# Time mixing of a two-layer model: from a scheduler's order to one written order for TensorE, VectorE, ScalarE and GpSimd

## The chip, the cores and the metric

The kernel runs on one core of a Trainium2 chip. The metric is the device time in microseconds (us) of one launch: 773.28 us is the median of three runs before the change (772.45, 773.28, 775.1). PE is TensorE, DVE is VectorE, ACT is ScalarE, POOL is GpSimd, and SP is the queue that issues the DMAs. A launch computes the whole model once, and all weights come from DRAM as float32 during it.

## The reference

The model has two layers over 256 tokens of width 1024 (16 heads of 64): layer 0 is block attention, layer 1 is RWKV-7 time mixing, each is followed by a gated feed-forward layer of width 2816, and a norm ends the program. The change is in time mixing only:

```python
xx = x_prev - x
xr, xw, xk, xv, xa, xg = [x + xx * mu[n] for n in range(6)]
r, k, v = xr @ w_r, xk @ w_k, xv @ w_v
w = -softplus(-(w0 + tanh(xw @ w1) @ w2)) - 0.5
decay = exp(-exp(w))
a = sigmoid(a0 + (xa @ a1) @ a2)
g = sigmoid(xg @ g1) @ g2
kk = k * k_k;  kk = kk / max(sqrt(sum(kk * kk)), 1e-12)     # per head
k = k * (1 + (a - 1) * k_a)
# per token t and head:
sa = state @ -kk_t
state = state * decay_t + outer(sa, kk_t * a_t) + outer(v_t, k_t)
y_t = state @ r_t
# then, per head
yn = (y - mean) * rsqrt(var + eps) * lnx_w + lnx_b
out = ((yn + sum(r * k * r_k) * v) * g) @ w_o
```

The kernel does not step through the tokens. It takes two chunks of 128 tokens, builds the triangular matrix T of products of decayed keys for every head and chunk, inverts I + T, and obtains the states and outputs by matrix products.

## The kernel before

Activations lie feature-major: a tile `x[:, kt]` is 128 features by 256 tokens, and there are eight of them. A weight piece of 128 x 1024 float32 (512 KB) is loaded by SP into `raw` and split exactly into a high and a low float32r part, the high one by ACT and the low one by DVE (`pieces`, `split_act`, both recorded as L133). A product with split operands is three matmuls (`mm3`, L137 to L139). Small projections run as plain float32 matmuls, which PE does in two passes; the trace has a record for each.

`rwkv` is the whole of time mixing. In the order of its code:

- for every contraction tile kt: the shifted and normed input `xn` (L449), its difference `xx` (L451), mixes of the two (L432), the key products (L137 to L139), the first halves of the low-rank projections for decay and rate (L463) and for the gate (L466), and the mixed value input;
- the second halves (L502, L503), the decays by a running sum (L510) and Exp (L587, L588), the key norms (squares L578, sums over a head L562, root L581, `spread` back over the head L569, directions L599), the products T (`prod`, L530, copied out by L533), the gate (L616), the values (L137 to L139, copied by L634);
- the inverses of 32 x 32 blocks of I + T: ACT and DVE gather the diagonal blocks (L649, L650), DVE transposes them (L651), and 31 steps of two DVE operations substitute (L655, L657), all heads and chunks at once;
- `state`: transposes back (L668, L670), scatters (L673, L674), corners of blocks of 32 and then of 64 (L683 to L715), means taken off the values (L726), X = M V (L747), token-major keys (L758), the two chunks (L768 to L789), the receptance r (L802, plain float32, 64 matmuls on unsplit weights), its products with keys (RK) and rates (RB) through `prod` with a mask (L536), the bonus (L822 to L835), the outputs (L852);
- `norm`, for two pairs of heads at a time: the remaining output products (L862 with U and RB, L864 with the state S1 and r), squares, sums, root, spread, gate and bonus, and a split; then the output projection.

A scheduler sets the order of instructions on each engine. It takes what is ready, and is guided by `issue_after` (do not place this before that) and by `weave`, which steps several generators in turn. Each engine then runs its own row strictly in that order. Weights of `wk` are loaded ahead during the last blocks of the feed-forward layer (`keys_ahead`).

Tiles come from pools with few slots: `b` has 15 general slots, `wp` 4 for split pieces, `rawp` 4, and PSUM has 4 slots `acc`, 2 `pt` and 2 `pu`. A writer waits until the slot's last reader is done.

Of the kernel before, what the change touches and what calls it, by code (L numbers as in the profile page):

```python
# [8 lines left out]
F32 = mybir.dt.float32  # L9
# [8 lines left out]
NB = 15  # L18
# [4 lines left out]
# columns of the packed vectors  # L23
# [8 lines left out]
# columns of the packed constants  # L32
# [31 lines left out]


class Trunk:
# [17 lines left out]
    def table(self, func, after):  # L84
        """have the activation table of func loaded once after is there, ahead of its use"""
# [14 lines left out]
    def t1(self, name="t1"):  # L100
        return self.wk.tile([128, S], F32, name=name, tag="t1", bufs=4)
# [12 lines left out]
    # ---- weights: raw float32 from DRAM, split exactly into two float32r parts  # L114
# [3 lines left out]
    def pieces(self, dram, n, own=0, after=False, fine=0):  # L118
        """dram [n/2, 128, 2048] -> n split pieces of [128, 1024], as a generator; the last own ones in general slots,
        the first fine ones in two steps"""  # L120
        for i in range(n):
            raw = self.raw()
            t = (self.b if i >= n - own else self.wp.tile)([128, 2, 1024], F32R, name="whl")
# [17 lines left out]
    # ---- the residual stream, feature-major; what the next sub-layer needs of it  # L141
# [28 lines left out]
    def rstd_tok(self):  # L170
        """1/rms of every token, tokens on partitions"""
# [12 lines left out]
    def rstd(self):  # L184
        """1/rms of every token, the same on all partitions (in PSUM)"""
# [7 lines left out]
    def out_proj(self, w, gname, split=True):  # L193
        """generator: h += w.T z; send (zhi, zlo) once per contraction tile"""
# [26 lines left out]
    # ---- layer 0: causal attention  # L221
# [15 lines left out]
    def attention(self, nxt="ffn0"):  # L237
# [55 lines left out]
        def soft(j):  # L293
            """heads 2j and 2j + 1"""
# [68 lines left out]
    # ---- gated convolutional feed-forward  # L363
    def ffn(self, l, nxt, split=True, ahead=iter(())):
# [30 lines left out]
        for fo in range(KT):  # L395
            ps = self.acc([128, S])
            for f in range(FT):
                if blk % 8 == 0:
                    hi, lo = next(w)
                    if blk >= 56 and blk % 16 == 8:  # L400
# [8 lines left out]
    # ---- layer 1: RWKV-7 time mixing  # L409
    def keys_ahead(self):  # L410
        for w in self.pieces(self.a["wk"], KT, own=KT, after=True):
            self.ahead.append(w)
            yield

    def rwkv(self, nxt="ffn1"):
        nc, a, tc = self.nc, self.a, self.tc
        mm = nc.tensor.matmul
        ident, head, sel = self.c("ident"), self.c("head"), self.c("sel", 0, 2)
# [3 lines left out]
        nc.sync.dma_start(l1[:, 1], a["g1"])  # L422
        omk = self.wk.tile([128, KT], F32, name="omk", bufs=1)
# [18 lines left out]
        # keys and the first halves of the low-rank projections, one contraction tile after the other  # L442
        xk = hilo()
        pk = []
        pwa, pg = self.pt([128, S]), self.pu([128, S])
        l2 = xv = None
        for kt in range(KT):
            with tc.issue_after(first[0].ins) if kt == 1 else nullcontext():
                nc.vector.scalar_tensor_tensor(xn[:, kt, 1:], self.h[:, kt], self.v("mix1", kt), rs,  # L449
                                               op0=OP.mult, op1=OP.mult)  # L450
            nc.vector.tensor_sub(xx[:, kt], xn[:, kt, :S], xn[:, kt, 1:])  # L451
            first = mix2(xk, 2, kt)
            for fo in range(KT):
                if kt == 0 and fo % 2 == 0:
                    pk.append(self.acc([128, 2, S]))
                f = slice(fo * 128, fo * 128 + 128)
# [7 lines left out]
            t = self.t1("mx")  # L464
            mix(t, 5, kt)
            mm(pg, lhsT=l1[:, 1, kt], rhs=t, start=kt == 0, stop=kt == 7)  # L466
            if kt == 0:
                l2 = self.b([128, 2, D], name="l2")
                nc.sync.dma_start(l2[:, 0], a["w2a2"])
                nc.sync.dma_start(l2[:, 1], a["g2"])  # L470
                xv = hilo()
            split = mix2(xv, 3, kt)
            if kt == 3:
                cut = split
        wv = self.pieces(a["wv"], KT)
        with tc.issue_after(cut[1].ins), tc.issue_after(cut[2].ins):
            wv0 = [next(wv) for _ in range(4)]

        # decay and in-context rate
        lt = self.wk.tile([128, S], F32, name="lt", bufs=1)  # L480
        nc.scalar.activation(lt[:64], pwa[:64], AF.Tanh)
        nc.scalar.copy(lt[64:], pwa[64:])
        gt = self.wk.tile([128, S], F32, name="gt", bufs=1)
        nc.scalar.activation(gt, pg, AF.Sigmoid)
        KK = self.b([128, KT, S], name="KK")
        for p in range(4):
            nc.vector.tensor_copy(KK[:, 2 * p:2 * p + 2], pk[p])
        A = self.b([128, KT, S], name="A")
        cm = self.b([128, KT, 2, C + 1], name="cm")
        nc.gpsimd.memset(cm[:, :, :, 0:1], 0.0)  # L490
# [497 lines left out]
```

## Time and profile before

| what | us |
|---|---|
| median of three runs (772.45 to 775.1) | 773.28 |
| span of the profiled execution, first to last instruction | 759.3 |
| the rest of the median | 13.98 |
| PE, DVE, ACT busy in the span | 725.8, 543.9, 389.4 |
| time mixing up to the last product T (327.6 to 399.9) | 72.3 |
| gates, values, gathers, substitution, first corners (399.9 to 449.81) | 49.9 |
| corners of 64 to the outputs (449.81 to 518.05) | 68.2 |
| norms and output projection (518.05 to 564.77) | 46.7 |

The stages are read from windows of the trace. "Busy" is time in which an engine has an instruction under way; a matmul that is slow because the clock is low or because its weights come late is busy all the same. [...] The chain of waits follows the work that ended last back through what released it, so an engine that appears there was on the path at that time.

### The profile page before, as it was taken

The numbers are of one execution on the slowest core, as the hardware profiler recorded it, in microseconds if no ns is written. First come the engines' busy times: TensorE is split into PE (matmuls) and PEld (weight loads), VectorE is DVE, ScalarE is ACT, GpSimd is POOL, SyncE is SP. The second block draws the span as 40 slices with busy tenths as digits, with TensorE's granted clock in tenths as the row PEclk, the third lists the DMA queues.
The fourth block names the chain that finished last, engine by engine and source line by source line (L and its number), as shares of the span: only waits on it lengthen the run. The fifth ranks groups of instructions, "written<-read, shape, count | busy, mean of one in ns | idle before, by whom it ended". The sixth has DMA issues, their size and how long they took to land. (4 is left out here: it accounts for less than half of the span.)

```text
span 759.3 us, 14375 instructions
## 1 busy us (share of the span) xinstructions
PE 725.8 (96%) x5924; PEld 664.3 (87%) x5924; DVE 543.9 (72%) x928; ACT 389.4 (51%) x657; POOL 16.9 (2%) x19
## 2 busy tenths in 40 slices
PE   6999999999999999989999789999999999999996
PEld 4777788999999999967777678877899999999995
DVE  5898766788887856679887984282868888886552
ACT  6566584655555555423684073231546555555541
POOL 0000000000000000000003000110000000000000
PEclk9999999999999999989999969999999999999998
DMA  8644435455555567813030304000335555555631
GB/s 291 223 127 135 151 118 165 138 171 191 178 183 188 177 216 254 298 63 100 13 106 20 126 30 139 2 29 2 115 108 191 175 190 195 175 188 184 196 120 55
DMA packets 30737, 108.70 MB, mean 143 GB/s; under 512 B 3408, under 2 KB 4048, under 8 KB 30672
## 3 DMA queue, kind: packets, MB, share of 16 engines
q1 hardware_dynamic: 30672, 107.79, 42.9%
q8 instruction: 46, 0.75, 0.4%
q14 instruction: 19, 0.16, 0.1%
HBM read 106.73 MB, written 1.05 MB: 142 GB/s over the span
## 5 line engine op out<-in xcount | busy, mean ns | idle before, releaser
L133 DVE TENSOR_TENSOR whl<-raw,whl 128x1024 fp32r<-128x1024 f32 (+1 forms) x189 | 228.9, 1217 | 87.3 <-ACT whl L133 87.1
L133 ACT CAST whl<-raw 128x1024 fp32r<-128x1024 f32 (+1 forms) x189 | 195.3, 1042 | 117.2 <-issue 55.4
L139 PE MATMUL acc<-xhi,whl 128*128 128x256 f32 x704 | 199.2, 283 | 0.0
L137 PE MATMUL acc<-xhi,whl 128*128 128x256 f32 x704 | 198.3, 282 | 0.0
L138 PE MATMUL acc<-xlo,whl 128*128 128x256 f32 x704 | 197.9, 281 | 0.0
L137 PEld LDWEIGHTS acc<-xhi,whl 128*128 128x128 f32 x704 | 133.7, 190 | 0.0
L138 PEld LDWEIGHTS acc<-xlo,whl 128*128 128x128 f32 x704 | 133.0, 189 | 0.2 <-DVE xlo L156 0.2
L139 PEld LDWEIGHTS acc<-xhi,whl 128*128 128x128 f32 x704 | 132.2, 188 | 0.0
L139 PE MATMUL acc<-hh,whl 128*128 128x256 f32 x352 | 99.0, 281 | 0.0
L137 PE MATMUL acc<-hh,whl 128*128 128x256 f32 x352 | 99.0, 281 | 0.0
L138 PE MATMUL acc<-hl,whl 128*128 128x256 f32 x352 | 98.9, 281 | 0.0
L137 PEld LDWEIGHTS acc<-hh,whl 128*128 128x128 f32 x352 | 66.4, 189 | 0.0
L138 PEld LDWEIGHTS acc<-hl,whl 128*128 128x128 f32 x352 | 66.3, 188 | 0.0
L139 PEld LDWEIGHTS acc<-hh,whl 128*128 128x128 f32 x352 | 66.3, 188 | 0.0
L133 ACT CAST hh<-ftmp 128x256 fp32r<-128x256 f32 x44 | 17.9, 406 | 55.0 <-DVE ftmp L389 55.0
L137 PE MATMUL acc<-whl,xhi 128*128 128x512 f32 x96 | 39.1, 414 | 6.0 <-ACT whl L133 6.0
L138 PE MATMUL acc<-whl,xhi 128*128 128x512 f32 x96 | 39.4, 410 | 0.8 <-DVE whl L133 0.8
L139 PE MATMUL acc<-whl,xlo 128*128 128x512 f32 x96 | 39.1, 407 | 0.0
L382 DVE TENSOR_TENSOR gb<-acc,rs 128x512 f32<-128x512 f32 x44 | 30.4, 691 | 8.5 <-PE acc L139 5.7
L802 PE MATMUL acc<-xr,raw 128*128 128x256 f32 x128 | 33.0, 418 | 0.0
L802 PEld LDWEIGHTS acc<-xr,raw 128*128 128x128 f32 x128 | 26.5, 211 | 4.4
L137 PEld LDWEIGHTS acc<-whl,xhi 128*128 128x128 f32 x96 | 18.6, 196 | 11.7 <-ACT whl L133 6.4
(243 smaller groups left out, 1225.4 us busy)
## 6 DMA issues: line engine op xcount, KB each, us to landing
raw<-wgu SPq DMA_DIRECT2D x88, 512.0 KB, 3.7
raw<-wd SPq DMA_DIRECT2D x44, 512.0 KB, 4.4
raw<-wqkv SPq DMA_DIRECT2D x23, 512.0 KB, 4.3
raw<-wo SPq DMA_DIRECT2D x16, 512.0 KB, 4.1
raw<-wk SPq DMA_DIRECT2D x8, 512.0 KB, 4.0
raw<-wv SPq DMA_DIRECT2D x8, 512.0 KB, 4.5
raw<-wr SPq DMA_DIRECT2D x8, 512.0 KB, 3.6
l<-g SPq DMA_DIRECT2D x2, 512.0 KB, 6.2
```

The lines of the kernel that those rows point to most:

```text
L133: return self.nc.scalar.copy(hi, src), self.nc.vector.tensor_sub(lo, src, hi.bitcast(F32))
L137: mm(out, lhsT=lh, rhs=rh, start=start, stop=False, skip_group_check=True)
L138: mm(out, lhsT=lh, rhs=rl, start=False, stop=False, skip_group_check=True)
L139: mm(out, lhsT=ll, rhs=rh, start=False, stop=stop, skip_group_check=True)
L382: nc.vector.tensor_mul(g[:, :, 2:], ps, rs[:, None, :].to_broadcast([128, 2, S]))
L802: mm(ps[:, e], lhsT=raw[:, kt * 128:kt * 128 + 128], rhs=xr[:, kt], start=kt == 0, stop=kt == 7)
```

## The change

Time mixing is written as functions (`lora`, `half`, `key`, `rates`, `decays`, `key_norms`, `values`, ...), and two functions, `order` and `order2`, call them one after the other. Both stand in a block that takes the order of PE, DVE, ACT and POOL as it is written. The norms and the output projection (`project`) stay with the scheduler. In particular:

- The first halves of the low-rank projections come before all keys. For decay and rate the mix is folded into the weights: `l1m` is l1 times mu, and the sum of l1·xn and l1m·xx takes two matmuls with 128 columns of weights (L459, L462) where there were two mixes and two matmuls with 64 columns. The gate's is L463.
- Keys are made in two halves: contraction tiles 0 to 3 for all eight output tiles, then 4 to 7 output tile by output tile. Each pair of output tiles (four heads) then gets its own norm, root and directions, while the keys of the next pair are made.
- The first piece of `wv` is laid ahead in the feed-forward layer; the others are split in two separate calls, `values_hi` on ACT and `values_lo` on DVE. Six of the sixteen half pieces of the values come between the products T, ten after them.
- Of the eight gathers ACT does six and DVE two; of the scatters DVE does five and ACT three.
- The 64 receptance products are dealt out by `fill`: 48 before the corners, 10, 5 and 1 among them.
- The heads go pair by pair through the corners of 64, X = M V, the chunks, RK, RB and the bonus.
- The bonus product over a head, one float32 matmul of 512 columns, becomes two float32r matmuls on a split input (L1010).
- The state's part of the outputs (S1 with r) is taken out of the norms and placed before them as one block.
- `b` has 17 slots and the ring `t1` 6 instead of 4; POOL clears the square tiles.

The core of the diff:

```diff
-            for i, n in enumerate((1, 4)):
-                t = self.t1("mx")
-                mix(t, n, kt)
-                o = slice(64 * i, 64 * i + 64)
-                mm(pwa[o], lhsT=l1[:, 0, kt, o], rhs=t, start=kt == 0, stop=kt == 7, skip_group_check=True)
+        def lora(kt):
+            nc.vector.scalar_tensor_tensor(xn[:, kt, 1:], self.h[:, kt], self.v("mix1", kt), rs,
+                                           op0=OP.mult, op1=OP.mult)
+            nc.vector.tensor_sub(xx[:, kt], xn[:, kt, :S], xn[:, kt, 1:])
+            mm(pwa, lhsT=l1[:, 0, kt], rhs=xn[:, kt, 1:], start=kt == 0, stop=False)
+            t = self.t1("mx")
+            mix(t, 5, kt)
+            mm(pwa, lhsT=l1m[:, kt], rhs=xx[:, kt], start=False, stop=kt == 7)
+            mm(pg, lhsT=l1[:, 1, kt], rhs=t, start=kt == 0, stop=kt == 7)
...
+        def order():
+            for kt in range(7):
+                lora(kt)
...
+            half(0)
+            mixes(xk, 2, (1, 2, 3, 4))
...
+            key(2, rest)
+            key(3, rest)
+            square_keys(1)
+            key_norms(0)
+            rate_keys(3)
+            inverse_norms(0)
+            mix_b()
+            rated(3)
+            key(4, rest)
+            directions(0)
...
+            prod(four(TT, 3), None, Bh, Kt, 3, (self.pt, self.pu))
+            gather(nc.scalar.copy, 0, range(4))
+            gather(nc.scalar.copy, 1, range(2))
+            values_hi(7)
+            values_lo(5)
+            receive(2, 8)
+            values_lo(6)
+            values_lo(7)
+            gather(nc.vector.tensor_copy, 1, range(2, 4))
+            nc.vector.transpose(GX[:, 0], tg)
+            for i in range(6, 2 * KT):
+                values(i // 2, i % 2)
+            substitute()
+            gates()
...
+        def bonus_end(p):
+            ps = self.acc([128, 2, S])
+            for i in range(2):
+                mm(ps, lhsT=headr, rhs=rks[p][i], start=i == 0, stop=i == 1)
...
+        def order2():
...
+            fill(48)
+            back(slice(0, 96), 0)
+            nc.vector.transpose(td, X)
+            corner32(0)
+            corner32(1)
...
+            for b in range(4):
+                outputs_state(b)
...
+        with tc.manual_schedule(engines={ET.PE, ET.DVE, ET.Activation, ET.Pool}):
+            order()
+            order2()
...
             def norm(b):
-                for j, c, o, hs, i, y, _ in outs(b):
-                    mm(y, lhsT=U[:, c, hs], rhs=RB[b // 2][:, i], start=False, stop=c == 0, skip_group_check=True)
-                    if c:
-                        mm(y, lhsT=S1[o, j], rhs=Rtf[o, j, C:], start=False, stop=True, skip_group_check=True)
+            outputs_pairs(b)
```

Three places of PE's row show how instructions move. The first is the opening of time mixing, behind the matmuls that spread the root mean square (L189). Before, a low-rank matmul (L463) comes first and the key products of tile 0 follow:

```order
L189 MATMUL pt<-con,rtok 128x128 x2
L463 MATMUL pt<-mx,l_3457 64x256
L137 MATMUL acc<-mhi,whl 128x256 x3
L138 MATMUL acc<-mlo,whl 128x256
L139 MATMUL acc<-mhi,whl 128x256
L137 MATMUL acc<-mhi,whl 128x256
```

Now, with `xn` and `xx` as direct inputs:

```order
L189 MATMUL pt<-con,rtok 128x128 x2
L459 MATMUL pt<-xn,l_3464 128x256
L462 MATMUL pt<-xx,l1m 128x256
L463 MATMUL pu<-mx,l_3464 128x256
L459 MATMUL pt<-xn,l_3464 128x256
L462 MATMUL pt<-xx,l1m 128x256
```

The low-rank matmuls stand in a block of 24 ahead of every key product.

The second place is around the corners. L802 before and L847 now are the receptance products, L683 and L882 the corners of 32, L707 and L906 those of 64 with L713 and L914 as their second halves. Before, from the values' last matmuls on, and then behind the corners of 32:

```order
L802 MATMUL acc<-xr,raw 128x256 x46
L683 MATMUL pt<-PN,sqr 32x32 x64
L802 MATMUL acc<-xr,raw 128x256 x5
...
L707 MATMUL pt<-PN,sqr 64x64 x16
L802 MATMUL acc<-xr,raw 128x256 x6
L713 MATMUL pu<-sqr,zs 64x64 x16
L707 MATMUL pt<-PN,sqr 64x64 x16
L802 MATMUL acc<-xr,raw 128x256 x2
```

Now:

```order
L847 MATMUL acc<-xr,raw 128x256 x48
L882 MATMUL pt<-PN,sqr 32x32 x64
L847 MATMUL acc<-xr,raw 128x256 x10
...
L847 MATMUL acc<-xr,raw 128x256 x5
L906 MATMUL pt<-PN,sqr 64x64 x16
L847 MATMUL acc<-xr,raw 128x256
L914 MATMUL pu<-sqr,zs 64x64 x8
L906 MATMUL pt<-PN,sqr 64x64 x8
```

Before, eleven receptance products stand behind the first corner of 64 (6, 2, 2 and 1); now one does.

The third place is the start of the norms. L862 before and L1040 now multiply U and RB, L864 and L1036 the state S1 and r, L562 and L539 are the sums, L569 and L546 the spreads. Before:

```order
L852 MATMUL acc<-sqr,V 64x128 x32
L862 MATMUL acc<-sqr,XS 64x128 x3
L864 MATMUL acc<-Rt,S_4748 64x128
L862 MATMUL acc<-sqr,XS 64x128
L864 MATMUL acc<-Rt,S_4748 64x128
L862 MATMUL acc<-sqr,XS 64x128 x3
L864 MATMUL acc<-Rt,S_4748 64x128
```

Now:

```order
L1036 MATMUL acc<-Rt,S_3525 64x128 x16
L1040 MATMUL acc<-sqr,XS 64x128 x13
L539 MATMUL pt<-con,sq 128x2 x4
L1040 MATMUL acc<-sqr,XS 64x128 x7
L546 MATMUL pu<-con,rn_5191 64x128 x8
L539 MATMUL pt<-con,sq 128x2 x4
```

The two kinds alternate before, and stand in blocks now.

## Rows read from the trace of the kernel before

**Rows 1.** The page's summary: busy time, share of the span, instructions.

```profile
span 759.3 us, 14375 instructions
...
PE 725.8 (96%) x5924; PEld 664.3 (87%) x5924; DVE 543.9 (72%) x928; ACT 389.4 (51%) x657; POOL 16.9 (2%) x19
```

**Rows 2.** Windows: stretch, length, then busy PE, PEld, DVE, ACT, POOL; PEclk, DMA.

```profile
200.00:322.00 122.00, 122.00 (x1023) 122.00 (x1022) 87.87 (x118) 65.07 (x91) 0.11 (x1) 1.00 0.65 216
...
324.10:330.90 6.80, 3.69 (x13) 2.57 (x14) 4.96 (x14) 2.51 (x5) 0.00 (x0) 0.52 0.31 125
...
327.60:399.90 72.30, 71.11 (x497) 56.53 (x499) 62.21 (x140) 39.05 (x73) 0.13 (x1) 0.98 0.18 59
449.81:518.05 68.24, 66.03 (x674) 57.40 (x675) 34.71 (x60) 22.46 (x40) 8.96 (x5) 0.92 0.14 48
...
450.40:457.20 6.80, 6.80 (x36) 5.80 (x35) 4.51 (x6) 3.28 (x6) 1.80 (x1) 0.51 0.07 14
511.80:515.20 3.40, 3.40 (x32) 3.18 (x34) 2.36 (x4) 0.00 (x0) 0.00 (x0) 0.54 0.00 0
...
518.05:564.77 46.72, 46.72 (x406) 40.09 (x400) 27.98 (x46) 21.44 (x40) 0.11 (x1) 1.00 0.28 91
```

**Rows 3.** Windows of the receptance matmuls (L802) alone.

```profile
412.00:431.80 19.80, 19.64 (x91) 17.41 (x92) 1.00 0.37 125
...
449.81:458.00 8.19, 5.13 (x12) 3.83 (x12) 0.58 0.16 30
458.00:500.00 42.00, 2.91 (x10) 1.66 (x10) 1.00 0.20 71
```

**Rows 4.** The chain of waits, 410 to 450: start, length, what.

```profile
410.07 1.26 DVE GX L651
...
411.43 0.22 DVE whl L655
...
434.79 0.59 DVE vm L726
435.38 1.82 DVE PN L668
437.34 3.64 PE pt L683 x128
...
449.81 3.04 PE pt L707 x32
```

**Rows 5.** The chain of waits, 499 to 526.

```profile
499.98 1.16 PE acc L530 x14
...
501.73 0.87 PE acc L830 x2
...
518.49 0.36 PE acc L864 x2
...
519.57 0.58 PE acc L862 x6
...
522.17 0.98 PE pt L562 x8
...
525.54 1.07 PE pu L569 x16
```

**Rows 6.** Groups by line and shape, 322 to 566: count, busy, mean ns, idle before.

```profile
L133 DVE TENSOR_TENSOR whl<-raw,whl 128x1024 fp32r<-128x1024 f32 x20 | 24.2, 1216 | 1.4 <-ACT whl L133 1.4
...
L599 DVE SCALAR_TENSOR_TENSOR KK<-KK,vec,pu 128x256 f32<-128x256 f32 x8 | 3.6, 472 | 3.0 <-PE pu L569 3.0
...
L602 DVE TENSOR_TENSOR A<-A,KK 128x512 f32<-128x512 f32 x4 | 2.7, 684 | 0.0
...
L133 ACT CAST whl<-raw 128x1024 fp32r<-128x1024 f32 x20 | 20.5, 1047 | 6.5 <-DMA raw<-wgu 5.3 <-PE acc L139 1.1
...
L649 ACT COPY whl<-sqr 32x512 f32<-32x512 f32 x4 | 4.4, 1093 | 1.2 <-PE acc L139 1.2
...
L533 ACT COPY sqr<-pu 128x512 f32<-128x512 f32 x4 | 2.4, 598 | 0.0
```

More of the change, by code (lines that the diff above doesn't have):

```diff
@@ L443, in rwkv, with key @@
         xk = hilo()
         pk = []
[L445 to L456, printed above, removed]
+        def key(fo, kts):
+            f = slice(fo * 128, fo * 128 + 128)
+            for kt in kts:
@@ L467, in rwkv @@
[L467 to L480, printed above, removed]
@@ new lines, in sums, with spread @@
+        def sums(dst, x):
+            for e in range(2):
+                for tt in range(2):
+                    mm(dst[:, tt, 2 * e:2 * e + 2], lhsT=x[:, e, tt * 128:tt * 128 + 128], rhs=sel,
+                       start=True, stop=True, skip_group_check=True)
+        def spread(ps, r):
+            for e in range(4):
+                for tt in range(2):
+                    mm(ps[e % 2 * 64:e % 2 * 64 + 64, e // 2, tt * 128:tt * 128 + 128],
+                       lhsT=r[:, tt, e:e + 1].to_broadcast([128, 64]), rhs=ident, start=True, stop=True,
+                       skip_group_check=True)
@@ new lines, in rwkv, with square_keys, key_norms @@
+        sqs, rns = {}, {}
+        def square_keys(p):
+            nc.scalar.copy(KK[:, two[p]], pk[p])
+            sqs[p] = self.t2("sq")
+            for e in range(2):
+                fo = 2 * p + e
+                nc.scalar.activation(sqs[p][:, e], KK[:, fo], AF.Square, scale=self.v("k_k", fo))
+        def key_norms(p):
+            pn = self.pt([128, 2, 4])
+            sums(pn, sqs[p])
+            rns[p] = self.wk.tile([128, 2, 4], F32, name="rn")
+            nc.scalar.activation(rns[p], pn, AF.Sqrt)
@@ new lines, in half, with mix_a, mix_b @@
+        def half(kt):
+            if kt == 0:
+                pk.extend(self.acc([128, 2, S]) for _ in range(4))
+            for fo in range(KT):
+                key(fo, (kt,))
+        pend = []
+        def mix_a(x, n, kt):
+            t = self.t1("mx")
+            mix(t, n, kt)
+            nc.scalar.copy(x[0][:, kt], t)
+            pend.append((x, kt, t))
+        def mix_b():
+            x, kt, t = pend.pop(0)
+            nc.vector.tensor_sub(x[1][:, kt], t, x[0][:, kt].bitcast(F32))
@@ L651, in rwkv @@
-        nc.vector.transpose(GX[:, 0], tg)
-        for j in range(31):
-            n, m = 31 - j, j + 1
-            t = tm[:, :n * m].rearrange("p (a b) -> p a b", b=m)
-            nc.vector.tensor_mul(t, GX[:, 0, j + 1:, j:j + 1].to_broadcast([128, n, m]),
-                                 X[:, j:j + 1, :m].to_broadcast([128, n, m]))
-            last = nc.vector.tensor_sub(X[:, j + 1:, :m], X[:, j + 1:, :m], t)
+            key(0, rest)
+            key(1, rest)
+            square_keys(0)
@@ new lines, in order @@
+            mix_b()
+            key(5, rest)
+            square_keys(2)
+            rates_of_keys(1)
+            key_norms(1)
+            inverse_norms(1)
+            key(6, rest)
+            mixes(xv, 3, (2, 3))
+            directions(1)
+            mix_b()
+            key(7, rest)
+            square_keys(3)
+            rates_of_keys(2)
+            key_norms(2)
+            inverse_norms(2)
+            mix_a(xv, 3, 4)
+            values(0, 0)
+            values_hi(4)
+            prod(four(TT, 0), None, Bh, Kt, 0, (self.pt, self.pu))
@@ L884, in state, with fill, zero @@
-            weave(norm(b) for b in range(4))
-            for j in range(8):
-                wo.send((zh[:, j], zl[:, j]))
-        with tc.issue_after(last.ins):
-            state()
+                        if e == 1 and kt == 7:
+                            nc.scalar.copy(Rtf[:, two[p]], ps)
+                        yield
+        rec = receptance()
+        def fill(n):
+            for _ in range(n):
+                next(rec, None)
+        def zero(x):
+            nc.gpsimd.memset(x, 0.0)
@@ new lines, in decayed, with moved, moved_end @@
+        def decayed(p):
+            nc.vector.tensor_mul(KE[:, two[p]], KE[:, two[p]], E2f[:, two[p]])
+        ms = {}
+        def moved(q):
+            ms[q] = [mt.next().rearrange("p (a b) -> p a b", a=4) for _ in range(2)]
+            prod(ms[q], "lt", Kh, Kt, q, (self.acc, self.acc))
+        def moved_end(q):
+            ps = self.pt([128, 2, 4, 64])
+            for k in range(4):
+                hs = slice((4 * q + k) * 64, (4 * q + k) * 64 + 64)
+                for c in range(2):
+                    mm(ps[:, c, k], lhsT=ms[q][k % 2][:, k // 2 * 2 + c], rhs=V[:, c, hs], start=True, stop=True)
+            nc.scalar.copy(XS[:, :, 256 * q:256 * q + 256], ps.rearrange("p c e v -> p c (e v)"))
```

727 lines of the change are left out of this document (435 added, 292 removed).

## The prediction

> **What bounds the kernel now.** I read the page's summary first: a span of 759.3 us and TensorE (PE) busy for 96% of it [rows 1]. The median of the runs is 773.28, so 13.98 us lie outside the span, and I leave them as they are. The stages by windows come next [rows 2]: in the feed-forward layers PE is busy all the time at full clock (1023 matmuls in 122.00 us, 0.119 us each for 256 columns in float32r), and the change can win nothing there. So I look only at time mixing, 327.6 to 564.8. In its first part (327.6 to 399.9: keys, decays, products T) PE is busy 71.11 of 72.30 us and VectorE 62.21; in its middle (449.81 to 518.05) PE is busy 66.03 of 68.24 at a mean clock of 0.92; in its last part (518.05 to 564.77) all of 46.72. A reader would stop here, since PE never seems to wait. But busy is not the same as needed, and three views show it. The granted clock falls to about 0.5, which is the 1.2 GHz level, in three of the windows of [rows 2], after stretches in which PE waited or ran small products. The chain of waits [rows 4] runs from 410.07 to 437.2 on VectorE alone (transpose, substitution, mean, transposes back), and PE waits for it. And the pieces of the chain in the last part [rows 5] show equal matmuls at unequal prices: that is worked out below.
>
> **The change, part by part.** A float32 matmul runs in two passes, each a record. 46 matmuls of L802 (92 weight loads recorded) took 19.80 us [rows 3], so 0.215 a record and 0.43 us a matmul of 256 columns. Per 512 columns float32r I take twice 0.119.
>
> Opening. After the change the low-rank parts come first: 8 times three f32 matmuls, 24 x 0.43 = 10.3, plus 2.2 because the clock is at its lower level there before too (6.8 us at 0.52 [rows 2], about a third of these matmuls). Then PE's own work, now in one row: 192 key products x 0.119 = 22.9; the second low-rank halves, 32 records on two halves of the rows, which I take to run side by side, 16 x 0.215 = 3.5 (6.9 if they don't); four sums x 0.98 = 3.9 and four spreads x 1.07 = 4.3 [rows 5]; four times 16 records of products T at 1.16 for 14 [rows 5], 5.2; six half pieces of values, 36 x 0.238 = 8.6. Sum 60.9. The first matmul needs only xn, not a mixed and split input, so I start it 1 us earlier, at 326.5. In a fixed order, what isn't covered is paid by everything behind it: each of four key norms goes sums 0.98, root and reciprocal about 0.6 with their waits, spread 1.07, then two L599 of 0.47 and two multiplications of 0.68 [rows 6], 5.0 in all, 20 for four. Between them stand key products of the next tiles, so I take 7 of the 20 (ends 0 and 20; the nearest row is before's own idle PE time in this stage, 72.30 - 71.11 = 1.2, but ScalarE gets more work in front of the first norm, so I stay above it). Last T product: 326.5 + 60.9 + 7 = 394.4, against 399.9.
>
> Gathers. Before, 399.9 to 411.43 = 11.5, four gathers on either engine. After, ScalarE does six and VectorE two: copies of T 2 x 0.60 = 1.2, six gathers x 1.09 = 6.6, the last piece of wv split behind them on ScalarE 1.05 and then VectorE 1.22, two gathers on VectorE at about 1 each, 2.0, transpose 1.26 [rows 4, 6], waits between about 1: 14.3. So this part loses 2.8. The substitution's 31 steps are the same, 434.79 - 411.43 = 23.4 [rows 4]; the mean (0.59) that stood between it and the transposes is moved behind. Transposes 1.8, start of the corners: 394.4 + 14.3 + 23.4 + 1.8 + 0.1 = 434.0, against 437.34. From there to the first corner of 64, 12.5 as before (449.81 - 437.34): scatters shift from ScalarE to VectorE, ten receptance products lie in the wait. So 446.5 against 449.81: **gain 3.3**. PE's wait before the corners is not a loss by itself; 48 receptance products (20.6), ten half pieces of values (14.3) and the gates (3.4) lie beside the gathers and substitution, 38.3 of some 39 us.
>
> Middle, 68.2 us before. Out of it go ten receptance products that before ran after 449.81: 12 records in 5.13 and 10 in 2.91 by busy time, 2.2 by pitch [rows 3]; one remains, 0.43: -6.9. The bonus product: 8 records, of which two took 0.87 [rows 5], 3.5, become 8 float32r products of 512 columns, 1.9: -1.6. In comes S1·Rt, 32 records, from the last part, at about 0.07: +2.2. What is left beyond need is idle PE (68.24 - 66.03 = 2.2) and the rest of the half clock (6.8 x 0.49 + 3.4 x 0.46 = 4.9, of which 2.5 went with the receptance products: 2.4) [rows 2]. Interleaved heads should take half of these 4.6: -2.3 (ends 0, and 4.6; and below nothing: with the fillers gone, up to 5 more of waits on VectorE's masked copies). Sum **gain 8.6**, 59.6 us.
>
> Last part, 46.7 before. U·RB (L862) has 128 rows of weights, S1·Rt (L864) 64, and they alternate. Six records of L862 take 0.58, four more than the 0.36 of two behind a change of shape: 0.055 a record, and a change of shape costs 0.25 [rows 5]. One norm's 24 records come as two runs of six and six of two, 2 x 0.58 + 6 x 0.36 = 3.3, four norms 13.3. After: 64 records of L862 together x 0.055 = 3.5; S1·Rt is counted in the middle. -9.8. In its place the first norm shows: square, sums 0.98, root, spread 1.07, three multiplications and a split before the first projection matmul, about 9 us, in which PE has 3.5 + 2.9 + 2.1 = 8.5 of work, and the later in-order waits about 1. I give 1.8 back: **gain 8.0** (ends 9.8 and 0).
>
> [...]
>
> Elsewhere: the early wv piece (1.05 on ScalarE, 1.22 on VectorE) and l1m (two VectorE multiplications of 512 columns, 0.68 each) lie under the first feed-forward, where PE is the bound [rows 2, 6]; if that cover failed, they would cost their durations. One table load less lies in ScalarE's slack. SP sends l2 behind four wv pieces; it is wanted only after the low-rank stage and a first eighth of the keys, some 16 us after the start.
>
> Sum: 3.3 + 8.6 + 8.0 = 19.9 us. On the profiled execution 739.4; on the median 773.28 - 19.9 = **753.4**.
>
> **Rivals.**
> (a) The order takes nearly all: opening waits 2 instead of 7, the middle 55 instead of 59.6: -9.6, 743.8. For: keys of the next tiles stand between the norms. Against: VectorE 62.21 of 72.30 in the opening has little slack. Chance 0.14.
> (b) The opening gains nothing and loses up to the norms' cost: 14 us of waits, 760.4. For: ScalarE's six gathers and its splits of wv stand in one queue. Chance 0.15.
> (c) The alternation wasn't what the norms cost, or their latency takes its place: no gain in the last part, 761.4. Chance 0.07.
> (d) The clock stays at 1.2 GHz for all the low-rank matmuls, of which each three get their inputs from three VectorE operations of about 0.47, 1.4 in all: 10.3 - 2.2 = 8.1 more, 761.5. For: they were at 0.52 before. Chance 0.07. [...]
> (e) Slower. The four key norms are hardly covered, since each engine keeps strictly to its row: with products T and copies behind each (1.3 + 0.6 + 0.6) a trip is 7.5, 30 for four, 23 more than I take; and the middle's 8.6 is lost to the same trips of the bonus (copy, multiply, split, product, multiply). All of it: 753.4 + 31.6 = 785. It is slower than before from 22.2, seven tenths of it. Against: 48 to 96 key products would have to stand idle beside. Chance 0.05.
>
> **How the numbers follow.** 0.3% of the time, 2.3 us, is what a measurement can tell from none. Forecast 0.52 (its own range 748 to 759), a 0.14, b 0.15, c 0.07, d 0.07, e 0.05. Faster: all but e and a bad sum of b, c and d, 0.92; within 0.3%: 0.03; slower: 0.05. The range 741 to 766 holds the forecast, a without its end, and b, c, d where they come singly.
>
> **What would show it.** The first low-rank matmul (L459) near 326.5 and 24 of them by 339; the last T product (L591) near 394, and if it is at 400 or later, (b). Substitution from 408 to 432. First L906 near 446.5. From there to the first L1040 about 60, without receptance products (L847) but one. The L1040 records at 0.055 and the last projection matmul some 38 us behind the first L1040; 46 would be (c). The granted clock in the low-rank stage tells (d). I am wrong in the whole if the waits of PE in the opening sum to over 20 us, or the feed-forward layers change.

## The result and the profile after

The changed kernel takes 739.38 us in the median (738.25 to 739.82, 4 runs) where the kernel before took 774.19 beside it: a ratio of 0.9533, with a 95% interval from 0.9495 to 0.9571. I forecast 753.4, faster by 19.9, in a range from 741 to 766. It is faster by some 35, so the direction is right and the size is not.

The first lines to read are the spans and mean granted clocks. Here are those of the profiled execution of before, of an ordinary execution of before that was profiled later (the fifth experiment), and of the changed kernel:

```profile
core 0: 759.3 us, clock 0.981
```

```profile
core 0: 771.6 us, clock 0.963
```

```profile
core 0: 737.3 us, clock 0.989
```

The execution behind [rows 1] was not an ordinary one. In every run whose span is on record the time is the span plus 1.7 to 1.9 us, so nothing like 13.98 us lies outside it; that execution itself took about 761. Of the 51 executions of before with a clock on record (42 beside the experiments and the nine of the fifth), eight were at 0.979 to 0.982 (760.8 to 763.5 us), one at 0.931 (797.0), and 42 at 0.955 to 0.965 (769.7 to 778.8). The profile I argued from is one of the minority, the median one of the rest.

By stages, all from windows of the three profiles:

| stage | before, profiled | before, ordinary | after | forecast |
|---|---|---|---|---|
| first corner of 64 starts at | 449.81 | 449.88 | 449.49 | 446.5 |
| middle (to the first U RB product) | 68.24 | 66.65 | 53.81 | 59.6 |
| last part (to the next norm's first sums) | 46.72 | 60.20 | 38.60 | 38.7 |
| the rest | 194.5 | 194.9 | 195.4 | unchanged |

The windows of the changed kernel, in the columns of [rows 2]; PEclk, the granted clock, is given there as a share of full clock:

```profile
326.13:338.72 12.59, 12.59 (x47) 10.66 (x48) 11.55 (x27) 1.35 (x2) 0.00 (x0) 0.79 0.00 1
326.13:395.84 69.71, 63.37 (x466) 55.75 (x468) 54.89 (x124) 37.31 (x82) 2.92 (x3) 0.94 0.09 31
436.69:449.49 12.80, 11.43 (x351) 9.85 (x352) 9.99 (x13) 7.80 (x11) 1.80 (x1) 1.00 0.24 80
449.49:503.30 53.81, 52.71 (x685) 47.54 (x686) 40.97 (x71) 23.75 (x41) 5.52 (x4) 1.00 0.14 44
503.30:541.90 38.60, 38.22 (x371) 36.33 (x371) 27.79 (x46) 21.24 (x40) 0.00 (x0) 1.00 0.37 119
```

The middle and the last part run at full clock from end to end, and PE has 1.1 us of idle time in the middle. The opening is as predicted in kind (the 24 low-rank matmuls begin at 326.1, the last of them at 338.7) and PE waits 6.3 us in it. The last part answers to [rows 2] and [rows 5]; the ordinary execution of before shows it very differently:

```profile
449.88:516.53 66.65, 64.44 (x674) 55.76 (x675) 34.59 (x60) 22.48 (x40) 8.96 (x5) 0.95 0.15 49
516.53:576.73 60.20, 60.20 (x404) 49.81 (x400) 28.19 (x46) 21.57 (x40) 0.11 (x1) 0.74 0.22 70
522.00:552.00 30.00, 30.00 (x153) 21.96 (x154) 9.97 (x17) 9.21 (x16) 0.11 (x1) 0.51 0.06 18
```

PE is busy in all of the 30 us from 522 to 552, at a clock of 0.51, and has 153 matmul records in them. In the execution that I had, the same 30 us held 266:

```profile
522.00:552.00 30.00, 30.00 (x266) 25.13 (x265) 18.67 (x27) 14.10 (x23) 0.11 (x1) 1.00 0.28 85
```

The profiles give the clock as a share only. Where the texts on record say 1.2 GHz, a share of 0.50 to 0.56 is what was measured. What it does to one product is seen in the opening of before, where the clock goes from 0.50 (329.7 to 330.9) to 1.00 (331.3 on) under key products of 256 columns (start, length, what):

```profile
330.57 0.41 PE L139 MATMUL acc<-mhi,whl 128*128 128x256 f32 x1
330.78 0.41 PE L138 MATMUL acc<-mlo,whl 128*128 128x256 f32 x1
331.00 0.35 PE L139 MATMUL acc<-mhi,whl 128*128 128x256 f32 x1
...
331.77 0.28 PE L137 MATMUL acc<-mhi,whl 128*128 128x256 f32 x1
331.89 0.28 PE L138 MATMUL acc<-mlo,whl 128*128 128x256 f32 x1
```

They start 0.21 us apart at the low clock, 1.2 columns a ns, and 0.12 apart at full clock.

The chain of waits of the ordinary execution shows where the low clock starts (start, length, what):

```profile
521.62 0.36 PE acc L862 x2
521.99 0.36 PE acc L864 x2
522.35 0.81 PE acc L862 x6
523.16 0.61 PE acc L864 x2
...
525.01 1.96 PE pu L569 x16
```

The alternating products of the norms run at the prices of [rows 5] for 6 us (0.36 for two), and from 522 on at 0.61; spreads take 1.96 where they took 1.07. In the changed kernel the same place, with S1 r in a block (L1036) and U RB together (L1040), reads:

```profile
501.40 1.89 PE acc L1036 x32
503.30 1.05 PE acc L1040 x16
504.43 0.61 ACT sq L1150
505.08 1.05 PE pt L539 x8
506.13 0.91 PE acc L1040 x13
507.15 0.87 PE pu L546 x15
...
513.19 1.07 PE pu L546 x16
```

0.059 a record in the block and 0.065 to 0.070 in U RB, against the 0.14 of before's mixed norms (3.3 for 24 records).

The waits of PE in time mixing after the change (waiting line, releaser, total, times, longest) show what the opening still lacks:

```profile
PE pu L546 <- DVE rn L570: 4.8, 2, 3.8
PE pt L539 <- ACT sq L557: 1.6, 1, 1.6
PE acc L847 <- issue: 1.4, 1, 1.4
PE pt L882 <- DVE PN L863: 1.3, 1, 1.3
```

The wait before the corners, L882 for PN, is 1.3; before it was 5.2:

```profile
PE pt L683 <- DVE PN L668: 5.2, 1, 5.2
```

A wait of 3.8 for the first inverse norm is new; and from the last product T the chain reads:

```profile
399.23 1.12 ACT whl L688
...
404.84 1.11 ACT whl L688
405.98 1.06 ACT whl L667
407.06 1.23 DVE whl L671
408.32 0.61 DVE whl L688
408.94 0.64 DVE whl L688
409.61 1.26 DVE GX L817
...
434.43 2.22 DVE PN L863
436.69 2.21 PE pt L882 x128
```

These are the steps of the prediction in its order: ScalarE's gathers, the last split on both engines, VectorE's gathers, transpose.

### The profile page after: what moved, and what is told of

It reads as the page before. It is cut to its first block, busy times and chain, and to the rows that moved or that the text cites. A ratio compares the mean times of both kernels' runs of the same rounds, so it can differ in the third digit from the quotient of the medians.

```text
span 737.3 us, 14365 instructions
## 1 busy us (share of the span) xinstructions
PE 704.4 (96%) x5924; PEld 655.3 (89%) x5924; DVE 541.2 (73%) x917; ACT 397.0 (54%) x675; POOL 16.8 (2%) x19
## 3 DMA queue, kind: packets, MB, share of 16 engines
HBM read 106.73 MB, written 1.05 MB: 146 GB/s over the span
## 4 chain that ended last, share of the span: by engine, by line
PE 67%; DVE 13%; DMA 9%; ACT 7%; issue 3%; SPq 1%; DVEq 0%; ACTq 0%
PE acc L137 17%; PE acc L139 17%; PE acc L138 17%; DMA raw<-wk 4%; DVE whl L133 3%; ACT whl L133 2%; DMA raw<-wqkv 2%; DMA raw<-wgu 2%; DVE GX L696 1%; DVE whl L694 1%; PE pu L546 1%; PE acc L847 1%; PE pt L591 1%; DMA l<-w1a 1%; PE pt L943 1%
## 5 line engine op out<-in xcount | busy, mean ns | idle before, releaser
L133 DVE TENSOR_TENSOR whl<-raw,whl 128x1024 fp32r<-128x1024 f32 (+1 forms) x182 | 220.6, 1218 | 88.8 <-ACT whl L133 88.5
L133 ACT CAST whl<-raw 128x1024 fp32r<-128x1024 f32 (+1 forms) x182 | 188.4, 1043 | 115.3 <-issue 54.7
L139 PE MATMUL acc<-whl,xlo 128*128 128x512 f32 x96 | 38.7, 403 | 0.0
L847 PE MATMUL acc<-xr,raw 128*128 128x256 f32 x128 | 28.8, 381 | 1.4 <-issue 1.4
L847 PEld LDWEIGHTS acc<-xr,raw 128*128 128x128 f32 x128 | 24.1, 190 | 4.8 <-issue 1.6
```

Of the source, the lines that this page charges most:

```text
L133: return self.nc.scalar.copy(hi, src), self.nc.vector.tensor_sub(lo, src, hi.bitcast(F32))
L139: mm(out, lhsT=ll, rhs=rh, start=False, stop=stop, skip_group_check=True)
L847: mm(ps[:, e], lhsT=raw[:, kt * 128:kt * 128 + 128], rhs=xr[:, kt], start=kt == 0, stop=kt == 7)
```

## Experiments

The clock decides so much here that each result names the clocks of its executions.

**1. The one setting that looked outside the span.** The kernel before with `dynamic_dma_scratch_size=2048` added:

```diff
-    nc = bacc.Bacc("TRN2", target_bir_lowering=False, num_devices=1)
+    nc = bacc.Bacc("TRN2", target_bir_lowering=False, num_devices=1, dynamic_dma_scratch_size=2048)
```

> The kernel before with the one setting dynamic_dma_scratch_size=2048 added, nothing else. The change took 22.0 us from the span and some 35 from the median, so about 13 us lay outside the span and went. Theory A: this setting (less memory set aside for dynamic DMAs) takes them: median near 761, span unchanged near 759. Rival B: they come from something else (the runs of before differ from its profiled execution, or the order of the instructions): median unchanged near 773 to 774.

Four executions took 760.8, 772.6, 774.1 and 797.7 us, at clocks of 0.981, 0.962, 0.963 and 0.931: the levels that the kernel before shows too, and no new one. Theory A falls. What the run gave instead is the list of spans, each some 1.8 us under its time, and with it the clock as the suspect.

**2. The states in a block, in the kernel before.**

```diff
+            for b in range(4):
+                for j, c, o, hs, i, y, first in outs(b):
+                    if c:
+                        mm(y, lhsT=S1[o, j], rhs=Rtf[o, j, C:], start=False, stop=False, skip_group_check=True)
...
                 for j, c, o, hs, i, y, _ in outs(b):
-                    mm(y, lhsT=U[:, c, hs], rhs=RB[b // 2][:, i], start=False, stop=c == 0, skip_group_check=True)
-                    if c:
-                        mm(y, lhsT=S1[o, j], rhs=Rtf[o, j, C:], start=False, stop=True, skip_group_check=True)
+                    mm(y, lhsT=U[:, c, hs], rhs=RB[b // 2][:, i], start=False, stop=True, skip_group_check=True)
```

> The kernel before with the products of S1 and r taken out of the norms and placed as one block of 16 ahead of U with RB, nothing else. Theory: a change between matmuls of 128 and of 64 weight rows costs 0.25 us, so the last part shrinks by about 8 (46.7 to 38 or 39) and the median by 6 to 8. Rival: the alternation was free and something else shortened the last part in the changed kernel: no change, within 2.

767.39 (766.37 to 768.7), a ratio of 0.9883 (0.9843 to 0.9922) to before: 9.4 us on a median of 776.8 in that set, where 6 to 8 was forecast. All four are at 0.961 to 0.964, as before is, but the profile has its long low stretch elsewhere, in the middle, and the last part runs at full clock:

```profile
471.00:498.00 27.00, 27.00 (x133) 25.07 (x134) 3.53 (x5) 5.28 (x9) 1.81 (x1) 0.50 0.07 20
531.50:570.93 39.43, 38.27 (x372) 36.40 (x371) 27.59 (x46) 21.49 (x40) 0.11 (x1) 1.00 0.32 108
```

The last part is 39.43 where it took 46.72 at full clock with the alternation: 7.3 less, of which the block of S1 r takes 1.89 back. These 5.4 are the alternation's own cost; the 9.4 of the medians also hold a low stretch that has another place and length. So taking the alternation out of the kernel before saves its own cost, and the clock then falls elsewhere. It is not the alternation alone that makes it fall in this kernel.

**3. The alternation, put back into the changed kernel.**

```diff
-                mm(y, lhsT=U[:, c, hs], rhs=RB[b // 2][:, i], start=False, stop=True, skip_group_check=True)
+                mm(y, lhsT=U[:, c, hs], rhs=RB[b // 2][:, i], start=False, stop=c == 0, skip_group_check=True)
+                if c:
+                    mm(y, lhsT=S1[o, j], rhs=Rtf[o, j, C:], start=False, stop=True, skip_group_check=True)
...
-            for b in range(4):
-                outputs_state(b)
```

> The changed kernel with the products of S1 and r put back between those of U and RB in the norms. Theory: the last part grows by about 8 as in the kernel before, median 739 to 746 or 747. Rival: nothing is lost, 739 to 740.

The median is 758.93, where 746 to 747 was forecast. One execution took 745.24 at 0.989: 5.9 more than the changed kernel, the forecast less 1 to 2. The three others took 758.8 to 763.3 at 0.962 to 0.972. The profile is of one of them (763.3):

```profile
505.48:560.00 54.52, 54.52 (x356) 44.55 (x354) 25.74 (x39) 17.92 (x31) 0.00 (x0) 0.72 0.28 92
513.00:543.00 30.00, 30.00 (x153) 22.91 (x154) 10.49 (x17) 10.18 (x17) 0.00 (x0) 0.50 0.10 34
```

It is the picture of the ordinary execution of before: full clock up to the norms, then 30 us at 0.50 with the same 153 matmuls in it. With the rest of the program as changed, the alternation is what makes the clock fall: in three executions of four by their mean clocks, with the place seen in the one profile. In the 23 executions of the changed kernel and of those variants of it that have neither alternation nor longer waits (experiments 7, 8, 9 and 11) the mean clock is 0.982 to 0.992.

**4. A longer wait before the corners.**

```diff
-            fill(48)
+            fill(38)
...
-            fill(10)
+            fill(20)
```

> The changed kernel with 38 instead of 48 receptance products ahead of the corners of 32 and 20 instead of 10 behind them: PE has 4.3 us less to do during the substitution and waits some 5.6 us before the corners, as the kernel before did. Theory: it is this wait after which the clock falls to 1.2 GHz in the corners of the kernel before; granted clock about 0.5 in the corner stage, and the middle starts 4 to 6 us later (the moved products 4.3, of which the scatters hide a part). Rival: the corners' small products themselves make the clock fall or not: granted clock stays 1.0, only the uncovered products cost, 0 to 4 us.

747.78 (745.62 to 751.72), 8.4 more than the changed kernel. PE's wait and the clock in the corners:

```profile
PE pt L882 <- DVE PN L863: 5.5, 1, 5.5
```

```profile
432.00:443.00 11.00, 6.92 (x136) 6.23 (x137) 10.45 (x16) 4.36 (x7) 0.00 (x0) 0.56 0.04 7
443.00:503.00 60.00, 57.85 (x811) 51.42 (x812) 37.16 (x66) 26.89 (x47) 7.23 (x4) 1.00 0.13 44
```

The wait of before is back, and with it a low clock in the corners (before's next one, from 450.4 on, is in [rows 2]). The theory holds in this profile, at a somewhat larger price: the first corner of 64 starts at 456.14 instead of 449.49, 6.7 later where 4 to 6 was forecast. And the new middle gets its full clock back at once.

**5. The kernel before, unchanged.**

> The kernel before, unchanged, for a profile of an ordinary execution: the seven timed ones lie at 772 to 779 us with a mean granted clock of 0.955 to 0.965, the profiled one that the prediction used had a span of 759.3 and 0.981. Theory: the missing 13 us are one more stretch at 1.2 GHz in the middle (as between 471 and 498 in the profile of the run with the states in a block), so the profile here shows a span of 770 to 775, a clock near 0.96, and a stretch of some 27 us at 0.50 between the corners of 64 and the chunks. Rival: the 13 us are spread over the program or lie in the feed-forward layers.

Eight of nine executions at 0.957 to 0.965 took 769.7 to 776.5, one at 0.982 took 760.76. The profile (shown above) has one more stretch at a low clock (0.51 from 522 to 552), as expected, but not between corners and chunks: it lies in the norms.

**6. The middle in stages, in the changed kernel.** The same calls of `order2`, in the order of the kernel before: X = M V, chunks, RK, bonus, RB, outputs.

```diff
-            moved_end(0)
-            moved_end(1)
-            moved(2)
-            bonus(0)
-            solve(0, 0)
...
+            moved_end(0)
+            moved(2)
+            moved_end(1)
...
+            for q in range(4):
+                pairs(RK, Kh, q)
+            for p in range(4):
+                bonus(p)
+                bonus_end(p)
```

> The changed kernel with the middle in the order of the kernel before: X = M V for all heads, then the chunks, then RK, bonus, RB and outputs, with the same instructions. Theory: it is the run of small products one behind the other (64 columns each, X = M V and chunks) after which the clock falls, and the new order pair by pair keeps it up; so the clock is at 0.50 for some 27 us behind 465 in most executions, and the time grows by 13 or more, to 752 and above, besides 2 to 6 us of uncovered waits (near 743 where the clock holds). Rival: the order of the heads only covers waits: granted clock stays at 1.0 there, 741 to 747.

757.19 (751.75 to 758.94) at clocks of 0.972 to 0.980. The size fits the theory, the place does not:

```profile
450.24:519.07 68.83, 58.14 (x684) 50.67 (x686) 42.40 (x72) 23.64 (x41) 7.14 (x5) 0.88 0.11 36
450.24:492.00 41.76, 38.98 (x504) 35.92 (x504) 22.32 (x39) 13.26 (x23) 7.03 (x4) 1.00 0.05 15
492.00:508.00 16.00, 8.80 (x31) 5.40 (x33) 11.05 (x21) 8.56 (x16) 0.00 (x0) 0.51 0.00 0
```

The middle is 68.83 long, 15.0 more than in the changed kernel. X = M V and the chunks, the long run of small products, keep the full clock. It falls in the bonus, where PE is idle 7.2 of 16 us: four round trips over ScalarE and VectorE, one behind the other. So here the order of the heads covers waits, and the clock is low where PE waits. That small products alone bring the clock down falls for this order. It is a stricter order than before's, though: PE idles 10.7 us in this middle, and 2.2 in before's.

**7. Gathers four and four.**

```diff
-            gather(nc.scalar.copy, 1, range(2))
...
-            gather(nc.vector.tensor_copy, 1, range(2, 4))
+            gather(nc.vector.tensor_copy, 1, range(4))
```

> The changed kernel with four gathers on ScalarE and four on VectorE as before, instead of six and two. The prediction had it that six on ScalarE with the last piece of wv behind them delay the substitution. Theory: ScalarE ends 2.2 earlier and VectorE has 1.2 to 2 more, so the substitution starts 0.2 to 1 earlier and the time is within 1 us of 739.4. Rival: ScalarE's row is the bound by itself, 2 us earlier, 737.

739.27 (737.52 to 741.48) against 739.38: within 1 us, as the theory said. The split of the gathers is worth nothing either way.

**8 and 11. The late activations moved forward.** In 8 they stand behind the second table load, in 11 ahead of the first (the diff is that of 11):

```diff
+            rate_keys(2)
+            rate_keys(3)
             self.table(AF.Exp, A[:, 7])
...
-            rate_keys(2)
...
-            rate_keys(3)
```

> The changed kernel with rate_keys(2) and rate_keys(3) (two activations each) moved ahead of the squares of the first pair, right behind the second table load. In the changed kernel VectorE waits 4.4 us for rate_keys(2), which stands behind square_keys(0), and PE then waits 3.8 us for the first inverse norm, after which the clock is at 1.2 GHz from 369 to 372. Theory: both waits go, the last product T comes 3 to 5 us earlier, and 735 to 737 follows, unless the gathers take it back. Rival: the waits are set by ScalarE's sum of work, and the moved activations only delay the squares: 739 to 741.

> The changed kernel with rate_keys(2) and rate_keys(3) ahead of the table load for Exp, where ScalarE waits for VectorE's mixes and decays anyway, instead of behind the squares. Theory: VectorE's wait for them (4.4) and PE's wait for the first inverse norm (3.8) go without delaying the squares; the last product T comes 4 to 5 us earlier, the corners 3 earlier; of this 1 to 3 us arrive at the end (in the run with them behind the second table load 3.1 at the substitution became 1.2 at the end): 736 to 738. Rival: the gain is taken back at the corners: 738 to 740.

738.2 (736.63 to 739.62, 5 runs) and 738.28 (736.33 to 740.77, 6 runs). In both the wait for the inverse norm falls from 3.8 to 1.0, but the wait for the squares rises from 1.6 to 3.5 (waits of PE in run 8; run 11 has the same two values):

```profile
PE pt L539 <- ACT sq L557: 3.5, 1, 3.5
...
PE pu L546 <- DVE rn L570: 1.0, 1, 1.0
```

The transposes back then end 3.1 and 1.9 earlier (433.6 and 434.7 against 436.7), and the median moves by 1.1 to 1.2, which these runs cannot tell from nothing. Forecasts of 735 to 737 for the one and 736 to 738 for the other were too good; the second lies in the range of its rival, by which the corners take the gain back. Neither is clearly better than the changed kernel.

**9. Two changes of shape a norm instead of eight.** `outputs_state(b)` directly ahead of `outputs_pairs(b)` in each norm.

```diff
-            for b in range(4):
-                outputs_state(b)
...
+            outputs_state(b)
             outputs_pairs(b)
```

> The changed kernel with the four S1 r products of each norm put directly ahead of its eight U RB products: two changes between 64 and 128 weight rows a norm instead of eight (alternating) or none. Theory: 0.25 us a change, 8 changes in all: +2 us, 741 to 742, and since there are few changes the clock holds (mean granted clock 0.98 or more in every execution). Rival: the clock falls whenever S1 r products stand among the norms at all: half or more of the executions near 0.97 and 755 to 760, as with alternation.

738.35 (736.96 to 740.08), all at 0.984 or more. The forecast of +2 was wrong, and no wait hides the changes: PE waits nowhere in these norms. The chain prices them:

```profile
502.23 0.58 PE acc L1036 x8
502.81 1.02 PE acc L1040 x16
```

Eight S1 r records take 0.58, four times, so 2.3 against the 1.89 of the block of 32; sixteen of U RB take 1.02, as in the changed kernel (1.05). The eight changes cost 0.4 together. So 0.25 a change, read from runs of two and six records, does not carry over to runs of eight and sixteen. The clock holds although the same products stand among the norms, so it is the constant change that matters in experiment 3, not where they stand.

**10. Receptance first, in the kernel before with the block of experiment 2.** The loop over L802 is placed ahead of the transposes back.

```diff
+            for p in range(4):
+                ps = self.acc([128, 2, S])
...
             # back: DT = transposed inverses, PN = the inverses as they are
```

> The kernel before with the states in a block (as in the second run) and all 64 receptance products ahead of the corners of 32, so that PE does not wait 5.2 us there (27.5 us of products beside 23.4 of substitution). In the second run, with the block alone, all four executions were at a clock of 0.961 to 0.964 and the profile had the clock at 1.2 GHz in the corners (435 to 447) and again from 471 to 498. Theory: both follow from PE's waits at the corners and their small products; without the long wait the corners run at full clock, the second stretch goes too in most executions, and the time is 750 to 755. Rival: the stretch from 471 comes from the work of the middle itself (masked copies, small products, the fillers now gone): clock near 0.97, 762 to 768.

788.89 (777.95 to 790.95) at clocks of 0.929 to 0.949: all four are above the slowest of the eleven executions of before beside them (777.8), and the median is 21.5 above that of experiment 2. Neither theory had that. PE no longer waits ahead of the corners, but inside them, with no receptance product left to run:

```profile
PE pu L703 <- ACT zs L697: 6.3, 1, 6.3
```

```profile
437.00:450.00 13.00, 10.85 (x169) 9.42 (x167) 12.48 (x22) 5.08 (x6) 1.80 (x1) 1.00 0.42 149
450.00:510.00 60.00, 52.70 (x492) 48.49 (x493) 22.26 (x34) 18.33 (x29) 4.67 (x3) 0.50 0.11 36
```

The clock is down for 60 us from there, and this is the fastest of the four executions.

**12. The same in the changed kernel.** `fill(64)` ahead of the corners, and no `fill` behind.

```diff
-            fill(48)
+            fill(64)
...
-            fill(10)
...
-            fill(5)
...
-            fill(1)
```

> The changed kernel with all 64 receptance products ahead of the corners of 32 and none among the corners (64 instead of 48, 10, 5 and 1). By time alone: 16 products (6.9 us) more ahead of the corners, where PE now waits 1.3, so the corners start some 5.5 later; the scatters then are partly done, and the 6.9 us behind are gone: 739 to 743. Theory from the run of the kernel before with receptance first: PE now waits inside the corners with nothing to do, the clock falls to 1.2 GHz there and stays low through the small products of the middle, 60 us in that run: 750 to 770 in most executions. Rival: the middle in its new order keeps the clock by itself (as it did after the wait before the corners in the fourth run): clock 0.97 or more, 739 to 747.

749.68 (746.48 to 753.42) at 0.968 to 0.979: between the two forecasts. The clock falls in the corners, but for a third of the time:

```profile
450.00:470.00 20.00, 19.18 (x335) 18.74 (x327) 7.45 (x12) 7.30 (x13) 3.61 (x2) 0.51 0.01 2
```

The wait ahead of it is 3.6 (L893 for the scattered `sqr`). From 470 to 505 the clock is 1.00 again. Dealing out 16 of 64 receptance products among the corners is worth about 10 us here.

## Why the prediction was wrong, point by point

**The step that failed is the first one:** "so 13.98 us lie outside the span, and I leave them as they are". All but the usual 1.8 of them lie inside the span of ordinary executions, as a stretch at a clock of 0.51 that the profiled one happened not to have. In the one ordinary profile it sits in the norms, where it adds 13.5 us (60.20 against 46.72); the whole span is 12.3 longer. The four executions of the changed kernel, at 0.982 to 0.991, have no such stretch (30 us at half clock would take 0.02 off the mean), so the change saves these 12 to 13 us as well. Against the profiled execution the change is worth 22.0 us of span, where I forecast 19.9; against the ordinary one 34.3. That 22.0 is so near 19.9 is partly luck: the opening gained 3.0 less than forecast and the middle 5.8 more. I had read the clock in windows and even priced its falls, but took one execution's clock for the kernel's. A span that is 14 us short of the median was the hint, and I passed over it.

**Opening and corners: forecast 3.3, measured 0.3.** The mechanism was right, most pieces a little too cheap. The last product T came at 395.84, not 394.4, since PE's own work took 63.4 and not 60.9 (the waits were 6.3 of the 7 taken). The second low-rank halves do run side by side, as I took them to: L497 and L498 start within 0.01 us of each other, 0.215 a pair. Then the chain to the end of the first transpose took 15.0 (395.84 to 410.87), not 14.3; the transposes back 2.22, not 1.8; and the way to the corners of 64 12.8, not 12.5. The wait I had placed at the first key norm is there, 3.8, with the clock at 0.50 from 369 to 372 behind it, and comes from an activation that stands behind the squares. Experiments 8 and 11 take it away and find the next wait behind it. Rival (b) was near: the opening gained almost nothing, though without the 14 us of waits.

**Middle: forecast 8.6, measured 14.4 (12.8 against the ordinary execution).** By busy time in the windows the receptance products are about as computed (8.04 to 0.70) and so is S1 r (1.96 in); the bonus gave 1.1 (4.20 to 3.13) and not 1.6. The term that was mis-sized is "half of these 4.6", and with it what was counted as left beyond need: the new order leaves 1.1 us of idle PE time and no low clock, rival (a)'s case, and products that I held for fixed need became cheaper. The largest group are the 192 products of keys, rates and r through `prod`, in the windows of the middle, before and after (busy PE and PEld, which is the weight loads, then PEclk and DMA):

```profile
449.81:518.05 68.24, 17.98 (x192) 15.12 (x192) 0.92 0.14 48
449.49:503.30 53.81, 13.70 (x192) 11.90 (x192) 1.00 0.14 44
```

That is 4.3 less for the same products. Little of it is the clock: in the ordinary execution, at full clock from 470 on, they take 17.39. Before, the chain from 497.3 to 511.6 runs mostly over VectorE (masked copies and bonus), which is busy 8.96 of the 9.05 us from 502.60 on, while PE gets 69 records into them. So some of PE's busy time was waiting too; this is read from the chain, and no run changes it alone. Experiment 6 shows what the order covers: the same instructions in stages take 68.83, with PE idle for 10.7. Experiments 4, 10 and 12 show that part of the gain is earned earlier: with waits of 5.5, 6.3 and 3.6 us at the corners the clock was 0.56 over 11 us, 0.50 over 60 and 0.51 over 20 there.

**Last part: forecast 8.0, measured 8.1 against the profiled execution, 21.6 against the ordinary one.** The alternation's own cost is confirmed by the last part of experiment 2 (5.4 net) and by the one execution of experiment 3 at full clock (5.9), and rival (c) is out. That 38.60 meets 38.7 so closely is luck in part: U RB took 0.065 to 0.070 a record and not 0.055, some 0.9 us more for 64, and the 1.8 given back for the norms was too much by about as much. In before's trace the weight loads of each new shape begin only with its own matmuls, after 0.17 us without a load:

```profile
518.77 0.19 PEld L862 LDWEIGHTS acc<-sqr,XS 128*64 128x64 f32 x2 [0.17 <-issue]
```

From 516 to 545 PEld idles so 28 times ahead of L862 and L864, 4.8 us in all: in this alternation of 128 and 64 rows no weight load of the next shape is seen beside the matmuls of the one before. What I did not see is that the alternation also brings the clock down (0.51 and 0.50 over 30 us in the profiles of experiments 5 and 3).

**Rival (d)**, the clock in the low-rank block, did not come: the mean is 0.79 from 326.13 to 338.72, low until about 331.5 and then full, which costs 2.6 where 2.2 was priced. **Rival (e)** did not come.

What stays open: why eight of some fifty executions of before keep their clock and the others do not, and why, without the alternation, the kernel before loses it in all four executions of experiment 2, in its one profile in the middle. Only one profile shows the place in an ordinary execution.

## What to carry to other kernels

Before a profile is used, compare its own execution time and mean granted clock with those of the timed runs; where they differ, look for the missing time in a second profile, not outside the span. Here the clock was 0.50 for 60 us with a wait of 6.3 us of TensorE at the corners (experiment 10) and 0.51 for 20 us with one of 3.6 (experiment 12), and matmuls that change their row count every time cost 5.9 us at full clock and 19.4 to 23.9 where the clock fell (experiment 3), so independent matmuls are best dealt out over the places where TensorE would wait, and products of one shape kept together. In an engine's fixed row a wait that is taken away can show the next one (from 3.8 to 1.0 for the inverse norm and from 1.6 to 3.5 for the squares, experiments 8 and 11): price the second before the first is counted as gain.

## What the runs showed of the hardware

In the norms of before, a matmul of 64 weight rows that alternates with one of 128 took 0.36 us for two records, where two took 0.11 to 0.14 without a change (L862 before, L1036 and L1040 after); in runs of eight and sixteen records (experiment 9) eight changes cost 0.4 in all. The kernel before had executions at two mean clocks with nothing changed, eight of 51 at 0.979 to 0.982 and 42 at 0.955 to 0.965; the longer stretches at a clock of 0.50 to 0.51 were 16 to 60 us in these profiles, with TensorE busy in 55 to 100% of them. Work of the same kind kept the full clock (1.00 from 450.24 to 492) where TensorE was busy in 38.98 of 41.76 us (X = M V and chunks in experiment 6), and stayed at the low one (0.50 from 450 to 510) when it began there (experiment 10).
